# A pinned order for the matmuls of a mixer, weights loaded earlier at the start, and a last norm without GpSimd

## The chip, the core and the metric

The program runs on one core of a Trainium2 chip, as one launch. Its engines are TensorE (PE for the products, PEld for loading their stationary operands), VectorE (DVE), ScalarE (ACT), GpSimd (POOL) and SyncE (SP), which issues most of the DMAs. The metric is the device time of one execution in microseconds (us). The median of three runs of the kernel before is 1447.36 us (1445.93 to 1447.79).

## The reference, cut to what matters

Two layers over 384 tokens (128 of a context group, 256 of a latent group), each layer a half SwiGLU FFN, a token mixer and another half FFN, each with an RMS norm and a shift, scale and gate that come from a condition vector by one matrix per layer. Only the first layer's mixer, the start and the final norm matter here.

```
def _gla_chunked(q, k, v, log_a, s0):            # chunks of 64 tokens, 4 heads, DK 64, DV 128
    b = cumsum(log_a); b_last = b[..., -1:]
    q_dec, k_inv, k_end = q*exp(b), k*exp(-b), k*exp(b_last - b)
    attn    = einsum('thk,shk->hts', q_dec, k_inv) * mask
    o_intra = einsum('hts,shv->thv', attn, v)
    delta   = einsum('shk,shv->hkv', k_end, v)   # the update of one chunk
    S, s_in = scan(S = decay*S + delta)          # the state that each chunk sees, from s0
    o_inter = einsum('thk,hkv->thv', q_dec, s_in)
    return o_intra + o_inter, S

def _gla_fnet_mixer(h, ...):
    q, k, v, og, lf, lb, u = split(h @ w_in)
    o  = rms(gla(forward) + gla(backward), g_head)      # mean over the 128 values of a head
    gla_out = o * silu(og)
    fn_out  = real(fft2(u, axes=(tokens, channels)))    # 4 groups of 128 channels
    return concat([gla_out, fn_out]) @ w_out, s_f, s_b

x = x + 0.5*gate*((silu(h @ w1) * (h @ w3)) @ w2)       # a half FFN, h = rms(x, g)*(1 + scale) + shift
y = rms(x, final_g)
```

## The kernel before, in words

Activations lie transposed, features on the 128 partitions and the 384 tokens along the free axis. A large product is made of three matmuls in a reduced float32 form (fp32r): weight and activation are each split into a high and a low part (`whi`, `wlo`, `hh`, `hl`; ACT makes the high part, DVE the low one), and high by high, high by low and low by high are added up in PSUM (`mm3` and `mm3x`, L345 to L355). Weights come from HBM in units of 1 MB (`raw`), in the order of one list; `load_to` issues the DMAs, `split_to` the split, `take` hands out the next unit. While a half FFN runs, DVE also works out the modulation vectors of later sub-layers by dot products (L151).

The start (L904 to L963) computes the first sub-layer's shift and scale in four quarters q. For each, 32 small matmuls (`mod<-raw_mod`, two tiles of 1 MB) give 512 sums, which are turned (`modt`), added to a bias and used to shift and scale two feature slices of x; those slices are then ready for the first products. Between the quarters stand products of the first two units of `w1` and `w3` (`ffn_p`, 8 slices k of 6 matmuls each), in an order written out in `fill` (L928). The PE order of this part is fixed (`manual_schedule`). x slices, `raw_mod` and the first three weight units share SP's queue.

The first mixer (`mixer_gla_fnet`, from L473) has the projections `in0`, `og`, `v`, `u`, then small matmuls in plain float32: the updates `delta` (L584: 40 of the first kind for ten pairs of chunk and direction, each in fact two passes, 64 rows deep), the scores `at` (L645), the two steps `fa` and `fb` of the Fourier transform (L618, L626), the outputs `o` of a block of 128 tokens (L663 and L669), and the mean of their squares `om` (L673). For each block ACT squares the outputs (`osq`, L671), `rsqrt` (L174 to L186: two ACT, then three DVE instructions on tiles `rs1`, `rs2`, `rs3`, of which `rs1` and `rs3` have one buffer) gives one over the root, and DVE multiplies by it and by the gate (L676, L678) and splits the result for the output projection `out0`. The states go from chunk to chunk by DVE (L597, L599). The order on every engine is set by a scheduler here, which interleaves pieces as it sees them become ready; PSUM has eight banks, from which `one_bank` and `two_banks` take in turn.

The end is `Last` (L239 to L275): the squares of slices 0 to 5 are added up on POOL (`ssq_final`), those of slices 6 and 7 go into the mean's matmuls separately (L267); `put` computes one over the root for the two token groups and multiplies x in pieces, some on DVE and two on POOL (L274), each with a DMA of its own (L275).

Of the kernel before, what the change touches and what calls it, by code (L numbers as in the profile page):

```python
# [9 lines left out]
F32 = mybir.dt.float32  # L10
# [35 lines left out]
def trunk(ctx, tc, a):  # L46
# [192 lines left out]
    class Last(Norm):  # L239
# [22 lines left out]
        def finish(self):  # L262
            terms = [self.ssq] + self.rest
            for c, t0, t1 in GROUPS:
                mean = one_bank(f"mean_final{c}")[:, : t1 - t0]
                for n, t in enumerate(terms):
                    pe.matmul(mean, lhsT=ones, rhs=t[:, t0:t1], start=(n == 0), stop=(n == len(terms) - 1))  # L267
                self.means.append(mean)

        def put(self, c, t0, t1, pieces):  # L270
            r = rsqrt(self.means[c], t1 - t0, f"final{c}")
            for n, (e, d0, d1) in enumerate(pieces):
# [72 lines left out]
    def mm3(out, wh, wl, mh, ml, start, stop):  # L345
        first = pe.matmul(out, lhsT=wh, rhs=mh, start=start, stop=False)  # L346
        pe.matmul(out, lhsT=wh, rhs=ml, start=False, stop=False)  # L347
        pe.matmul(out, lhsT=wl, rhs=mh, start=False, stop=stop)  # L348
        return first
# [8 lines left out]
    def products(pp, u, by_tile=False):  # L358


        for m, k in [(m, k) for k in range(KD) for m in range(2)] if by_tile else [(m, k) for m in range(2) for k in range(KD)]:
            wh, wl = u[m]
            mm3x(pp[:, m], wh[:, k], wl[:, k], k)
# [109 lines left out]
    def mixer_gla_fnet(l, feed, make_next):  # L473
        with tc.tile_pool(name="mix0", bufs=1) as mp, tc.tile_pool(name="mix0w", bufs=2) as mw:
# [32 lines left out]
            for dr in range(2):  # L507
                for pr in range(2):
# [16 lines left out]
                    df = mw.tile([P, T], F32, tag="ke", name=f"df{nm}")  # L525
# [43 lines left out]
            def channels(i):  # L569
                uu.append(tmp.tile([P, 2, T], F32, tag="ev", name=f"u{i}"))  # L570
                project(("u0", i), feed, uu[i], f"u0_{i}")
# [5 lines left out]
            def advance(c, dr, to):  # L577
                t, hf = c // 2, c % 2
                pd = one_bank(f"delta{c}{dr}")
                rows = slice(64 * hf, 64 * hf + 64)  # L580
                for pr in range(2):
                    for par_ in range(2):
                        hd = 2 * pr + par_
                        pe.matmul(  # L584
                            pd[64 * par_ : 64 * par_ + 64, pr * P : pr * P + P],
                            lhsT=kt[rows, t, dr, pr, 64 * par_ : 64 * par_ + 64],
                            rhs=v[rows, t, hd * P : hd * P + P], start=True, stop=True,
                        )
                if to is None or c in (0, 1):
                    s = mp.tile([P, 2, P], F32, name=f"s{c}{dr}")  # L590
                else:
                    s = st[:, 3 * dr + (c - 2) % 3]
                prev = s_in.get((dr, c))
                for pr in range(2):
                    cols = slice(pr * P, pr * P + P)
                    if prev is None:
                        dve.tensor_copy(s[:, pr], pd[:, cols])  # L597
                    else:
                        dve.scalar_tensor_tensor(  # L599
                            s[:, pr], prev[:, pr], dec[dr, pr][:, c : c + 1], pd[:, cols], op0=ALU.mult, op1=ALU.add  # L600
                        )
                if to is not None:
                    s_in[dr, to] = s
                return s
# [10 lines left out]
            def fourier(g):  # L615
# [3 lines left out]
                y = mw.tile([P, 3, 256], F32, tag="fy", name=f"fy{g}", bufs=1)  # L619
                act.copy(y[:, :2].rearrange("p t c -> p (t c)"), pa[:, :512])  # L620
                dve.tensor_tensor(y[:, 2], y[:, 1], pa[:, 512:768], op=ALU.subtract)
                dve.tensor_tensor(y[:, 1], y[:, 1], pa[:, 512:768], op=ALU.add)
                pb = one_bank(f"fb{g}")[:, :T]
# [13 lines left out]
            def scores(t):  # L637
# [12 lines left out]
                w2 = mw.tile([P, 4, P], F32, tag="as", name=f"as{t}")  # L650
# [4 lines left out]
            def attend(t, am):  # L655
                ts = slice(t * P, t * P + P)
                po = two_banks(f"o{t}")
                sq = tmp.tile([P, 2, 256], F32, tag="rs3", name=f"osq{t}", bufs=1)
                todo = [(dr, c) for c in (2 * t, 2 * t + 1) for dr in range(2) if (dr, c) in s_in]
                for pr in range(2):  # L660
                    for par_ in range(2):
                        hd = 2 * pr + par_
                        pe.matmul(po[:, par_, pr * P : pr * P + P], lhsT=v[:, t, hd * P : hd * P + P], rhs=am[:, 2 * par_ + pr],  # L663
                                  start=True, stop=not todo, skip_group_check=True)
                    for n_, (dr, c) in enumerate(todo):
                        o0 = pr * P + (c % 2) * 64
                        for par_ in range(2):
                            rows = slice(64 * par_, 64 * par_ + 64)
                            pe.matmul(po[:, par_, o0 : o0 + 64], lhsT=s_in[dr, c][rows, pr], rhs=qd[dr, pr][rows, c * 64 : c * 64 + 64],  # L669
                                      start=False, stop=(n_ == len(todo) - 1), skip_group_check=True)  # L670
                act.activation(sq, po[:, :, :256], AF.Square)  # L671
                pm = one_bank(f"om{t}")
# [8 lines left out]
            def deltas():  # L681
                for i in range(3):
                    advance(2 + i, 0, 3 + i)
                    advance(5 - i, 1, 4 - i)
                    if i == 0:
                        advance(0, 0, 1)
                        advance(1, 1, 0)
                    if i == 1:
                        nc.sync.dma_start(a["sf"], advance(1, 0, None))
                        nc.sync.dma_start(a["sb"], advance(0, 1, None))  # L690
# [12 lines left out]
            fourier(2)  # L703
            attend(2, am[2])
            fourier(3)
# [200 lines left out]
    with tc.tile_pool(name="boot", bufs=1) as bp, tc.manual_schedule(engines={mybir.EngineType.PE}):  # L906
        raw_mod = {}
        for q in range(4):
# [4 lines left out]
            load_to(min(q + 1, 2))  # L913
# [3 lines left out]
        def begin(ft, ks):  # L917
# [9 lines left out]

        fill = (((), ((0, (0, 1)),)), ((), ((0, (2, 3)), (1, (0, 1)))), (((1, (2,)),), ((1, (3,)), (0, (4, 5)))), (((1, (4,)),), ((1, (5,)), (0, (6, 7)), (1, (6, 7)))))  # L928
        for q in range(4):
# [8 lines left out]
            row = bp.tile([P, P], F32, name=f"modrow0_{q}")  # L938
            dve.tensor_copy(row, acc)
            for args in fill[q][0]:  # L940
                begin(*args)
            pt = one_bank(f"modt0_{q}")
            pe.transpose(pt[:, :P], row, ident)
# [11 lines left out]
            if q < 2:  # L955
                split_to(q + 1)
            for d in (2 * q, 2 * q + 1):
                feed.add(d)
            for args in fill[q][1]:
                begin(*args)  # L960
# [11 lines left out]
    last.put(*GROUPS[0], ((dve, 0, 4), (pool, 4, 8)))  # L972
    last.put(*GROUPS[1], ((dve, 0, 2), (pool, 6, 8), (dve, 2, 4), (dve, 4, 6)))
# [147 lines left out]
```

## Time and profile before

| | us |
|---|---|
| median of three runs | 1447.36 |
| profiled execution | 1448.87 |
| its span | 1446.0 |
| PE busy | 1412.8 (98%) |
| DVE busy | 1086.2 (75%) |
| ACT busy | 599.2 (41%) |
| POOL busy | 125.1 (9%) |

The profiled execution is 2.87 us longer than its span, and 1.51 us longer than the median. PE is busy for almost the whole span, so a stretch of time in which PE waits is what can be seen at once; a wait of another engine matters only where PE waits for that engine in turn. The granted clock is one in most of the span and a half in a few short stretches.

### The profile page before, as it was taken

The numbers are of one execution on the slowest core, as the hardware profiler recorded it, in microseconds if no ns is written. First come the engines' busy times: TensorE is split into PE (matmuls) and PEld (weight loads), VectorE is DVE, ScalarE is ACT, GpSimd is POOL, SyncE is SP. The second block draws the span as 40 slices with busy tenths as digits, with TensorE's granted clock in tenths as the row PEclk, the third lists the DMA queues.
The fourth block names the chain that finished last, engine by engine and source line by source line (L and its number), as shares of the span: only waits on it lengthen the run. The fifth ranks groups of instructions, "written<-read, shape, count | busy, mean of one in ns | idle before, by whom it ended". The sixth has DMA issues, their size and how long they took to land.

```text
span 1446.0 us, 21500 instructions
## 1 busy us (share of the span) xinstructions
PE 1412.8 (98%) x8508; PEld 1371.4 (95%) x8508; DVE 1086.2 (75%) x1815; ACT 599.2 (41%) x976; POOL 125.1 (9%) x98
## 2 busy tenths in 40 slices
PE   6999999999999999999999999999999999999996
PEld 4999999999889999999999999999876999999996
DVE  3799889879876888888879888885667675666433
ACT  4543443335344443433344344333248444344332
POOL 2000000012102000000100000011145200000001
PEclk9999999999999999999999999999989999999998
DMA  9666657563414456556636565664320234433331
GB/s 394 233 212 206 226 185 243 214 218 110 154 47 144 147 198 209 195 188 222 225 132 238 200 204 190 215 219 156 121 85 1 103 132 150 142 131 125 124 103 44
DMA packets 48515, 245.26 MB, mean 170 GB/s; under 512 B 5376, under 2 KB 9856, under 8 KB 29088
## 3 DMA queue, kind: packets, MB, share of 16 engines
q1 hardware_dynamic: 44560, 240.80, 47.6%
q10 hardware_dynamic: 3856, 3.10, 0.7%
q8 instruction: 66, 1.08, 0.3%
q14 instruction: 33, 0.27, 0.1%
HBM read 241.79 MB, written 2.10 MB: 169 GB/s over the span
## 4 chain that ended last, share of the span: by engine, by line
PE 95%; DVE 2%; ACT 1%; DMA 1%; issue 0%; DVEq 0%; SPq 0%; ACTq 0%
PE ffn_p L353 17%; PE ffn_p L355 17%; PE ffn_p L354 17%; PE ffn_acc L346 8%; PE ffn_acc L348 8%; PE ffn_acc L347 8%; PE out_acc L348 2%; PE out_acc L346 2%; PE out_acc L347 2%; PE attn L796 1%; PE av L871 1%; PE attn L851 1%; DMA raw_mod<-in_modw 1%; PE mod L934 1%; PE attn L353 0%; DVE wlo L214 0%
## 5 line engine op out<-in xcount | busy, mean ns | idle before, releaser
L213 ACT CAST whi<-raw 128x1024 fp32r<-128x1024 f32 (+2 forms) x317 | 324.7, 1027 | 609.1 <-PE ffn_p L354 279.9
L214 DVE TENSOR_TENSOR wlo<-raw,whi 128x1024 fp32r<-128x1024 f32 (+2 forms) x317 | 377.8, 1195 | 167.1 <-ACT whi L213 166.3
L353 PE MATMUL ffn_p<-hh,whi 128*128 128x388 f32 x1408 | 478.4, 340 | 4.6 <-ACT whi L213 3.0
L355 PE MATMUL ffn_p<-hh,wlo 128*128 128x386 f32 x1408 | 475.1, 337 | 1.1 <-DVE wlo L214 1.1
L354 PE MATMUL ffn_p<-hl,whi 128*128 128x384 f32 x1408 | 472.7, 336 | 0.2
L151 DVE SCALAR_TENSOR_TENSOR junk<-modw,cb 128x1024 f32<-128x1024 f32 x256 | 314.3, 1228 | 2.1
L353 PEld LDWEIGHTS ffn_p<-hh,whi 128*128 128x128 f32 x1408 | 265.0, 188 | 6.5 <-ACT whi L213 3.2
L355 PEld LDWEIGHTS ffn_p<-hh,wlo 128*128 128x128 f32 x1408 | 265.8, 189 | 2.7 <-DVE wlo L214 2.6
L354 PEld LDWEIGHTS ffn_p<-hl,whi 128*128 128x128 f32 x1408 | 264.6, 188 | 1.4 <-DVE hl L235 1.0
L346 PE MATMUL ffn_acc<-gh_ffn,whi 128*128 128x384 f32 x704 | 236.8, 336 | 0.0
L348 PE MATMUL ffn_acc<-gh_ffn,wlo 128*128 128x384 f32 x704 | 236.7, 336 | 0.0
L347 PE MATMUL ffn_acc<-gl_ffn,whi 128*128 128x384 f32 x704 | 236.7, 336 | 0.0
L203 POOL TENSOR_TENSOR ssq_n<-ssq_n,sq_n 128x384 f32<-128x384 f32 x42 | 59.7, 1423 | 894.0 <-ACT sq_n L202 869.6
L347 PEld LDWEIGHTS ffn_acc<-gl_ffn,whi 128*128 128x128 f32 x704 | 132.4, 188 | 0.0
L346 PEld LDWEIGHTS ffn_acc<-gh_ffn,whi 128*128 128x128 f32 x704 | 132.4, 188 | 0.0
L348 PEld LDWEIGHTS ffn_acc<-gh_ffn,wlo 128*128 128x128 f32 x704 | 132.4, 188 | 0.0
L434 DVE TENSOR_TENSOR ffn_e<-ffn_p,r_n 128x768 f32<-128x768 f32 x88 | 84.0, 955 | 49.1 <-PE ffn_p L355 48.9
L85 ACT ACTIVATE ffn_e<-ffn_e,ffn_wb 128x128 f32<-128x128 f32 (+1 forms) x176 | 70.4, 449 | 51.8 <-DVE ffn_wb L368 51.5
L214 DVE TENSOR_TENSOR gl_ffn<-ffn_e,gh_ffn 128x384 fp32r<-128x384 f32 x88 | 49.0, 557 | 37.6 <-ACT gh_ffn L213 37.4
L213 ACT CAST gh_ffn<-ffn_e 128x384 fp32r<-128x384 f32 x88 | 45.0, 511 | 62.3 <-DVE ffn_e L438 61.8
L438 DVE SCALAR_TENSOR_TENSOR ffn_e<-ffn_e,ffn_wb 128x128 f32<-128x128 f32 (+1 forms) x176 | 65.0, 411 | 0.0
L235 DVE SCALAR_TENSOR_TENSOR hl<-x,mods,hh 128x128 fp32r<-128x128 f32 (+1 forms) x96 | 57.3, 637 | 2.0 <-ACT hh L234 1.2
(261 smaller groups left out, 1256.2 us busy)
## 6 DMA issues: line engine op xcount, KB each, us to landing
raw<-in_w SPq DMA_DIRECT2D x120, 1024.0 KB, 4.8
modw<-in_modw SPq DMA_DIRECT2D x128, 512.0 KB, 3.4
raw<-in_w SPq DMA_DIRECT2D x16, 768.0 KB, 4.9
raw_mod<-in_modw SPq DMA_DIRECT2D x8, 1024.0 KB, 15.3
raw<-in_w_in SPq DMA_DIRECT2D x8, 1024.0 KB, 4.8
raw<-in_w_out SPq DMA_DIRECT2D x8, 1024.0 KB, 4.8
raw<-in_w_og SPq DMA_DIRECT2D x2, 1024.0 KB, 4.7
raw<-in_w_v SPq DMA_DIRECT2D x2, 1024.0 KB, 4.8
```

Source lines behind the costliest of these rows:

```text
L85: i = act.activation(out, in_, func, **kw)
L151: i = dve.scalar_tensor_tensor(junk, raw, 1.0, cb[:, c], op0=ALU.mult, op1=ALU.mult, accum_out=mods[l][v][:, d, c : c + 1])
L213: i = act.copy(hi, src).ins
L214: pace["last"] = dve.tensor_tensor(lo, src, f(hi), op=ALU.subtract).ins
L346: first = pe.matmul(out, lhsT=wh, rhs=mh, start=start, stop=False)
L347: pe.matmul(out, lhsT=wh, rhs=ml, start=False, stop=False)
L348: pe.matmul(out, lhsT=wl, rhs=mh, start=False, stop=stop)
L353: first = pe.matmul(out[:, :TX], lhsT=wh, rhs=hh[:, k, :TX], start=(k == 0), stop=False)
L354: pe.matmul(out[:, :T], lhsT=wh, rhs=hl[:, k], start=False, stop=False)
L355: pe.matmul(out[:, :TM], lhsT=wl, rhs=hh[:, k, :TM], start=False, stop=(k == KD - 1))
L434: dve.tensor_tensor(e, pp[:, :, :T], feed.r.unsqueeze(1).broadcast_to([P, 2, T]), op=ALU.mult)
L438: dve.scalar_tensor_tensor(e[:, 1, t0:t1], e[:, 1, t0:t1], wb[:, 1, c : c + 1], e[:, 0, t0:t1], op0=ALU.add, op1=ALU.mult)
```

## The change

Three places are changed. In the first mixer the PE order is written out and pinned: matmuls of one form stand in runs; all 40 updates stand in one run, between the two halves of the second `u` unit, and take turns between the upper and lower 64 rows; the state chain on DVE follows as one piece; the outputs of blocks 0 and 1 share one pair of PSUM banks (`o01`), and block 2 has another; the Fourier steps are two functions (`by_channel`, `by_token`), and so are the squares and the gate (`squares`, `gated`). The tiles of `df` move to another tag, and the masked scores of the last block take an `rs2` tile. At the start the second unit's weights are loaded right behind the first's, ahead of x's second quarter, and the products are put in another order. At the end slice 6 joins POOL's sum of squares, the means stand behind the last products, and all final multiplications are DVE's.

```
# the end
         def add(self, d):
-            if d < KD - 2:
+            if d < KD - 1:
...
-                    pe.matmul(mean, lhsT=ones, rhs=t[:, t0:t1], start=(n == 0), stop=(n == len(terms) - 1))
+                    i = pe.matmul(mean, lhsT=ones, rhs=t[:, t0:t1], start=(n == 0), stop=(n == len(terms) - 1))
+                    after(i.ins, pace["product"], "the last products before the means")
...
-                e.tensor_tensor(xs, xs, r.unsqueeze(1).broadcast_to([P, d1 - d0, t1 - t0]), op=ALU.mult)
+                dve.tensor_tensor(xs, xs, r.unsqueeze(1).broadcast_to([P, d1 - d0, t1 - t0]), op=ALU.mult)
...
-    last.put(*GROUPS[0], ((dve, 0, 4), (pool, 4, 8)))
-    last.put(*GROUPS[1], ((dve, 0, 2), (pool, 6, 8), (dve, 2, 4), (dve, 4, 6)))
+    last.put(*GROUPS[0], ((0, 4), (4, 8)))
+    last.put(*GROUPS[1], ((0, 2), (2, 4), (4, 6), (6, 8)))
# the mixer
+            def channels(i, between):
                 uu.append(tmp.tile([P, 2, T], F32, tag="ev", name=f"u{i}"))
-                project(("u0", i), feed, uu[i], f"u0_{i}")
+                u = take(("u0", i))
+                pp = two_banks(f"u0_{i}")
+                half(pp, u, 0)
+                between()
+                half(pp, u, 1)
+                spread(uu[i], pp, feed, f"u0_{i}")
+                pump()
...
+                for n in range(0, len(steps), 2):
+                    for pr in range(2):
+                        for par_ in range(2):
+                            for c, dr, to in steps[n : n + 2]:
+                                t, hf = c // 2, c % 2
+                                rows = slice(64 * hf, 64 * hf + 64)
...
-                w2 = mw.tile([P, 4, P], F32, tag="as", name=f"as{t}")
+                if t < 2:
+                    w2 = mw.tile([P, 4, P], F32, tag="as", name=f"as{t}")
+                else:
+                    w2 = tmp.tile([P, 4, P], F32, tag="rs2", name=f"as{t}")
...
-            turn_values(0, vts[0])
-            channels(0)
-            turn_values(1, vts[1])
-            deltas()
-            am = [scores(0), scores(1)]
-            fourier(0)
-            fourier(1)
-            channels(1)
-            attend(0, am[0])
-            am.append(scores(2))
-            attend(1, am[1])
-            fourier(2)
-            attend(2, am[2])
-            fourier(3)
+            with tc.manual_schedule(engines={mybir.EngineType.PE}):
+                turn_values(0, vts[0])
+                channels(0, lambda: turn_values(1, vts[1]))
+                am[0] = scores(0)
+                channels(1, deltas)
+                am[1] = scores(1)
+                am[2] = scores(2)
+                for g in range(2):
+                    y[g] = by_channel(g)
+                pair = two_banks("o01")
+                po[0], po[1] = pair[:, :, :256], pair[:, :, 256:]
+                for t in range(2):
+                    attend(t, am[t], po[t])
+                po[2] = two_banks("o2")[:, :, :256]
+                attend(2, am[2], po[2])
+                for g in range(2):
+                    by_token(g, y[g])
+                gated(0, po[0], squares(0, po[0]))
+                gated(1, po[1], squares(1, po[1]))
+                for g in range(2, 4):
+                    y[g] = by_channel(g)
+                gated(2, po[2], squares(2, po[2]))
+                for g in range(2, 4):
+                    by_token(g, y[g])
# the start
-            load_to(min(q + 1, 2))
+        load(0)
+        load_to(2)
+        for q in range(1, 4):
+            load(q)
         load_to(3)
...
+        sums(0)
+        apply(0)
+        split_to(1)
+        begin(0, 0, 1)
+        split_to(2)
+        begin(1, 0, 1)
+        sums(1)
+        apply(1)
+        sums(2)
+        begin(0, 2)
+        apply(2)
+        begin(0, 3)
+        begin(1, 2, 3)
+        sums(3)
+        begin(0, 4)
+        apply(3)
+        begin(0, 5)
+        begin(1, 4, 5)
+        begin(0, 6, 7)
+        begin(1, 6, 7)
         split_to(3)
```

Below is what the order of instructions says of three places. The first is DVE around the states of the first mixer, before (`at` and `delta` are PSUM tiles of scores and updates, `am` and `as` the masked scores, `states` and `s` the states).

```order
L214 TENSOR_TENSOR wlo_1024_3637<-raw_3331,whi_1024_3636 128x1024
...
L599 SCALAR_TENSOR_TENSOR states<-c_s0f,dec_3029,delta_3489 128x128
...
L649 TENSOR_TENSOR am_3574<-at_3565,c_mask 128x512
L597 COPY s_3508<-delta_3503 128x128 x2
...
L651 TENSOR_TENSOR as_3576<-at_3565,c_mask 128x512
L599 SCALAR_TENSOR_TENSOR states<-states,dec_3029,delta_3519 128x128
...
L649 TENSOR_TENSOR am_3588<-at_3579,c_mask 128x512
...
L651 TENSOR_TENSOR as_3590<-at_3579,c_mask 128x512
```

And the same stretch of DVE now, from the first masked scores to the last.

```order
L680 TENSOR_TENSOR am_3498<-at_3489,c_mask 128x512
L685 TENSOR_TENSOR as_3500<-at_3489,c_mask 128x512
L151 SCALAR_TENSOR_TENSOR junk,mods_7_99<-modw_7_6_3638,cb 128x1024 x2
L214 TENSOR_TENSOR wlo_0_3861<-raw_3421,whi_0_3860 128x1024
L626 SCALAR_TENSOR_TENSOR states<-c_s0f,dec_3029,delta_3539 128x128
...
L380 TENSOR_TENSOR u_3503<-u_1_3514,r_n_2934 128x768
...
L214 TENSOR_TENSOR wlo_1024_3865<-raw_3421,whi_1024_3864 128x1024
...
L680 TENSOR_TENSOR am_3651<-at_3642,c_mask 128x512
L685 TENSOR_TENSOR as_3653<-at_3642,c_mask 128x512
L680 TENSOR_TENSOR am_3665<-at_3656,c_mask 128x512
L685 TENSOR_TENSOR as_3667<-at_3656,c_mask 128x512
```

The scores of blocks 1 and 2 (`at_3642`, `at_3656`) are masked behind the whole state chain, the second `u` unit and the split of two weight tiles; before, blocks 0 and 1 were masked between the steps of the chain.

The second place is PE around the means of squares of the first mixer, before (`osq` are the squared outputs, `fy` the result of the first Fourier step).

```order
L618 MATMUL fa_3781<-c_cc,u_3631 128x256 x3
L673 MATMUL om_3767<-osq_3745,ones_h 128x512
L626 MATMUL fb_3789<-c_cs_p,fy_3785 128x128 x2
L663 MATMUL o_3800<-as_3741,v_3106 128x128 x2
L626 MATMUL fb_3789<-c_cs_s,fy_3785 128x128 x4
...
L618 MATMUL fa_3837<-c_cc,u_3631 128x256 x2
L673 MATMUL om_3823<-osq_3801,ones_h 128x512
L618 MATMUL fa_3837<-c_cc,u_3631 128x256
L346 MATMUL out_acc_3865<-fh,whi_1024_3636 128x384
```

And now.

```order
L657 MATMUL fb_3751<-c_cs_s,fy_3682 128x128 x4
L711 MATMUL om_3764<-osq_3762,ones_h 128x512
L711 MATMUL om_3781<-osq_3779,ones_h 128x512
L646 MATMUL fa_3795<-c_cc,u_3503 128x256 x3
L646 MATMUL fa_3803<-c_cc,u_3503 128x256 x3
L711 MATMUL om_3813<-osq_3811,ones_h 128x512
L657 MATMUL fb_3827<-c_cs_p,fy_3799 128x128 x2
L657 MATMUL fb_3827<-c_cs_s,fy_3799 128x128 x4
L347 MATMUL out_acc_3859<-fh,whi_1024_3508 128x384
```

The three means stand almost together, the first two with nothing between them; before, score, output and Fourier matmuls stood between one mean and the next.

The third place is PE at the end of the program, before.

```order
L348 MATMUL ffn_acc_12491<-gh_ffn_10406,wlo_1024_12553 128x384
L267 MATMUL mean_final_12653<-ssq_final,ones 128x128
L267 MATMUL mean_final_12657<-ssq_final,ones 128x256
L267 MATMUL mean_final_12653<-sq_final_12624,ones 128x128
L346 MATMUL ffn_acc_12491<-gh_ffn_10406,whi_0_12548 128x384
...
L267 MATMUL mean_final_12657<-sq_final_12624,ones 128x256
L267 MATMUL mean_final_12653<-sq_final_12648,ones 128x128
L267 MATMUL mean_final_12657<-sq_final_12648,ones 128x256
```

And now.

```order
L349 MATMUL ffn_acc_12485<-gh_ffn_10400,wlo_1024_12547 128x384
L267 MATMUL mean_final_12647<-ssq_final,ones 128x128
L267 MATMUL mean_final_12650<-ssq_final,ones 128x256
L267 MATMUL mean_final_12647<-sq_final_12642,ones 128x128
L267 MATMUL mean_final_12650<-sq_final_12642,ones 128x256
```

All matmuls of the mean stand behind the last product, and there are four of them in place of six.

## Rows read from the trace of the kernel before

**Rows 1.** The page: shares of the span of the chain that ended last, by engine.

```profile
PE 95%; DVE 2%; ACT 1%; DMA 1%; issue 0%; DVEq 0%; SPq 0%; ACTq 0%
```

**Rows 2.** PE in order of time, the mixer: start, length, instruction, idle time before it.

```profile
376.46 0.82 PE L554 MATMUL vt<-ident,vT 128*128 128x128 f32 x6
...
400.42 0.61 PE L663 MATMUL o<-as,v 128*128 128x128 f32 x4
...
403.55 1.13 PE L673 MATMUL om<-osq,ones_h 128*128 128x512 f32 x2 [0.20 <-ACT osq L671]
...
408.79 1.53 PE L618 MATMUL fa<-c_cc,u 128*128 128x256 f32 x6
410.16 1.02 PE L673 MATMUL om<-osq,ones_h 128*128 128x512 f32 x2
...
452.88 0.34 PE L353 MATMUL ffn_p<-hh,whi 128*128 128x388 f32 x1
```

**Rows 3.** DVE in order of time, the same stretch.

```profile
377.61 1.22 DVE L214 TENSOR_TENSOR wlo<-raw,whi 128x1024 fp32r<-128x1024 f32 x1
378.74 1.02 DVE L376 TENSOR_TENSOR u<-u,u_wb 128x256 f32<-128x256 f32 x2
379.68 0.60 DVE L599 SCALAR_TENSOR_TENSOR states<-c_s0f,dec,delta 128x128 f32<-128x128 f32 x2
...
389.16 1.22 DVE L151 SCALAR_TENSOR_TENSOR junk<-modw,cb 128x1024 f32<-128x1024 f32 x1
...
406.76 0.68 DVE L649 TENSOR_TENSOR am<-at,c_mask 128x512 f32<-128x512 f32 x1
```

**Rows 4.** ACT in order of time, the first block's squares and root.

```profile
404.77 0.69 ACT L85 ACTIVATE lnv_o<-om,eps 128x512 f32<-128x512 f32 x1 [1.28 <-PE om L673]
...
409.34 0.60 ACT L671 ACTIVATE osq<-o 128x512 f32<-128x512 f32 x1 [3.21 <-DVE r_o L186]
```

**Rows 5.** POOL in order of time, the masked scores' sums.

```profile
387.17 1.27 POOL L652 TENSOR_TENSOR as<-as,am 128x512 f32<-128x512 f32 x1 [3.03 <-DVE as L651]
```

**Rows 6.** Stretches: length; PE, PEld, DVE, ACT, POOL busy; clock; DMA share, GB/s.

```profile
1043.00:1045.70 2.70, 0.95 (x12) 0.57 (x8) 2.70 (x3) 0.00 (x0) 2.27 (x2) 0.99 0.00 0
1045.70:1052.50 6.80, 6.45 (x18) 5.43 (x19) 4.09 (x6) 1.58 (x9) 2.54 (x2) 0.50 0.46 157
...
1072.80:1076.40 3.60, 0.26 (x2) 0.26 (x4) 3.60 (x10) 2.44 (x7) 1.26 (x1) 1.00 0.63 264
1076.40:1079.80 3.40, 3.40 (x14) 1.62 (x14) 2.87 (x12) 1.84 (x7) 2.67 (x3) 0.50 0.00 0
```

**Rows 7.** PE in order of time, the start.

```profile
30.55 1.95 PE L934 MATMUL mod<-raw_mod,cs 128*32 128x128 f32 x64
...
46.69 0.34 PE L353 MATMUL ffn_p<-hh,whi 128*128 128x388 f32 x1
46.87 0.34 PE L354 MATMUL ffn_p<-hl,whi 128*128 128x384 f32 x1
...
48.23 0.45 PE L355 MATMUL ffn_p<-hh,wlo 128*128 128x386 f32 x1 [0.50 <-DVE wlo L214]
```

**Rows 8.** SP's DMA issues in order of time, the start.

```profile
8.14 2.26 SPq L912 DMA_DIRECT2D raw_mod<-in_modw  x2
```

**Rows 9.** The tile raw_mod, its DMAs' times from issue to landing.

```profile
DMA to landing us min/median/max: 6.4/15.3/18.0
```

**Rows 10.** All engines in order of time, the end.

```profile
1429.05 0.82 PE L267 MATMUL mean_final<-ssq_final,ones 128*128 128x128 f32 x4
...
1430.30 0.42 PE L346 MATMUL ffn_acc<-gh_ffn,whi 128*128 128x384 f32 x1
...
1436.86 1.71 POOL L274 TENSOR_TENSOR x<-x,r_final 128x512 f32<-128x512 f32 x1 [22.88 <-ACT r_final L85]
...
1437.82 1.04 DVE L185 SCALAR_TENSOR_TENSOR u_final<-u_final,r_final 128x256 f32<-128x256 f32 x1
...
1439.35 2.96 DVE L274 TENSOR_TENSOR x<-x,r_final 128x512 f32<-128x512 f32 x3
```

More of the change, by code (lines that the diff above doesn't have):

```diff
@@ L347, in mm3 @@
         pe.matmul(out, lhsT=wh, rhs=ml, start=False, stop=False)
-        pe.matmul(out, lhsT=wl, rhs=mh, start=False, stop=stop)
+        pace["product"] = pe.matmul(out, lhsT=wl, rhs=mh, start=False, stop=stop).ins
         return first
@@ L362, in products, with half @@
             wh, wl = u[m]
+            mm3x(pp[:, m], wh[:, k], wl[:, k], k)
+    def half(pp, u, m):
+        wh, wl = u[m]
+        for k in range(KD):
             mm3x(pp[:, m], wh[:, k], wl[:, k], k)
@@ L507, in mixer_gla_fnet @@
             for dr in range(2):
+                kes = mw.tile([P, 2, T], F32, tag="fy", name=f"df{dr}")
                 for pr in range(2):
@@ L524, in mixer_gla_fnet @@
                     bl = b6[:, :, 0:1] if dr else b6[:, :, 63:64]
-                    df = mw.tile([P, T], F32, tag="ke", name=f"df{nm}")
+                    df = kes[:, pr]
                     pool.tensor_tensor(df.rearrange("p (c t) -> p c t", c=6), bl.broadcast_to([P, 6, 64]), b6, op=ALU.subtract)
@@ L575, in mixer_gla_fnet @@
             s_in = {(0, 2): cst["s0f"], (1, 5): cst["s0b"]}
[L577 to L597, printed above, removed]
-                    else:
[L599 to L604, printed above, removed]
@@ L622, in fourier, with by_token @@
                 dve.tensor_tensor(y[:, 1], y[:, 1], pa[:, 512:768], op=ALU.add)
+                return y
+            def by_token(g, y):
                 pb = one_bank(f"fb{g}")[:, :T]
@@ L653, in scores, with attend @@
                 return w2
[L655 to L658, printed above, removed]
+            def attend(t, am, po):
                 todo = [(dr, c) for c in (2 * t, 2 * t + 1) for dr in range(2) if (dr, c) in s_in]
@@ L663, in attend @@
                         pe.matmul(po[:, par_, pr * P : pr * P + P], lhsT=v[:, t, hd * P : hd * P + P], rhs=am[:, 2 * par_ + pr],
-                                  start=True, stop=not todo, skip_group_check=True)
+                                  start=True, stop=False, skip_group_check=True)
                     for n_, (dr, c) in enumerate(todo):
@@ L670, in attend, with squares, gated @@
                                       start=False, stop=(n_ == len(todo) - 1), skip_group_check=True)
+            def squares(t, po):
+                sq = tmp.tile([P, 2, 256], F32, tag="rs3", name=f"osq{t}", bufs=1)
                 act.activation(sq, po[:, :, :256], AF.Square)
+                return sq
+            def gated(t, po, sq):
+                ts = slice(t * P, t * P + P)
                 pm = one_bank(f"om{t}")
@@ L906, in trunk, with load @@
     with tc.tile_pool(name="boot", bufs=1) as bp, tc.manual_schedule(engines={mybir.EngineType.PE}):
-        raw_mod = {}
-        for q in range(4):
+        raw_mod, rows = {}, {}
+        def load(q):
             nc.sync.dma_start(x[:, 2 * q : 2 * q + 2], a["xT"][:, 2 * q : 2 * q + 2])
@@ L925, in begin, with sums @@
                     mm3x(begun[ft][:, i], wh[:, k], wl[:, k], k)
-        fill = (((), ((0, (0, 1)),)), ((), ((0, (2, 3)), (1, (0, 1)))), (((1, (2,)),), ((1, (3,)), (0, (4, 5)))), (((1, (4,)),), ((1, (5,)), (0, (6, 7)), (1, (6, 7)))))
-        for q in range(4):
+        def sums(q):
             acc = one_bank(f"mod0_{q}")[:, :P]
@@ L937, in trunk, with apply @@
                         )
[L938 to L941, printed above, removed]
+            rows[q] = bp.tile([P, P], F32, name=f"modrow0_{q}")
+            dve.tensor_copy(rows[q], acc)
+        def apply(q):
             pt = one_bank(f"modt0_{q}")
-            pe.transpose(pt[:, :P], row, ident)
+            pe.transpose(pt[:, :P], rows[q], ident)
             for v in range(2):
```

56 lines of the change are left out of this document (37 added, 19 removed).

## The prediction

> **What bounds the kernel now.** I read the chain that ended last first: 95% of it is PE's [rows 1], so the end moves by what PE's stream gains or loses, and by the short stretches at the two ends where PE has nothing to do. The second view is PE in order of time through the first mixer. It shows hardly a gap: 0.20 us before the first mean of squares is the kind of wait to be found there, though the chain from one mean to the next is long. From the first `om` to the second are 410.16 - 403.55 = 6.6 us [rows 2], in which PE does scores, outputs and a Fourier step. The scheduler had put work there. Third, DVE in the same stretch, since the new order makes PE wait for it [rows 3], and ACT's part of the root [rows 4]. Fourth, the stretches with the granted clock, for what happens after PE has been idle. Last, the start and the end, where the page's share of PE says nothing.
>
> **The mixer up to the outputs.** PE does the same until the first `vt`. Its second one (0.82 us long, of which 0.75 hold up what follows, [rows 2]) now stands inside the first `u` unit, so DVE has that unit 0.75 us later: its last additions, 378.74 to 379.68 before [rows 3], end at 380.4. What DVE then does is fixed by its order. Two masks of the first scores at 0.60 (a 512-wide one is 0.68 long and overlaps the next by some 0.08) bring it to 381.6; two dots and one weight split, each 1.13 to 1.15 from start to start (377.61 to 378.74), to 385.05. Then the chain: 16 multiply-adds at 0.26 (two in 0.52, 0.60 long) and four copies, which I take at 0.2, end at 390.0. The second `u` unit's scaling with the weight split and the additions behind it takes what the first's took, 3.1 us from the product's end (376.46, by the `vt` behind it) to 379.68 less the latency: 393.1. Masks of block 1: 394.3. The masked part of block 2 needs the single `rs1` tile, which POOL reads for 1.27 us [rows 5]: 395.6, and two masks more: 396.8.
>
> PE is ahead of that. By the runs' own durations it has done the scores of block 2 and the first `fa` by 392.5. The second `fa` takes over the PSUM bank of block 1's scores and waits for 394.3: 1.9 us idle. The outputs' bank pair takes over that of block 2's scores: PE is free at 395.7 and waits until 397.0 with the semaphore: 1.3 us. So whatever PE saves by runs of one form before 397.0, it waits away; the shorter updates gain nothing. Outputs began at 400.42 before and at 397.0 now.
>
> **The mixer from there.** Before, 452.88 - 400.42 = 52.5 us led to the next FFN [rows 2]. Of these 0.5 us were waits and 1.3 us the scores of block 2, which now lie earlier; 2.4 us of `fb` for two groups, which stood among the products of `u`, come in. So 53.1 us of work, and I take 0.3 us off for fewer changes of form (0 to 1.5: the outputs keep their alternation of forms, so little is left to save).
>
> The Trainium skill, "TensorEngine Tiling (Array Packing)", section Key Properties, says that a change of the tiling mode drains TensorE, by which each change taken out should pay. It does here too, but those taken out lie mostly ahead of the wait that ends at 397.0.
>
> Now the waits. The first `om` waits 0.15 us for a PSUM bank. The second stands directly behind it, and its squares on ACT wait for DVE's last reading of block 0's output: `rs3` has one buffer. Before, that chain took 6.6 us with two masks of 0.60 inside, so 5.4; the squares waited for the third instruction of the root (409.34, [rows 4]) and now for the product behind it, 0.7 us more: 6.1 us from `om` to `om`. The mean itself is 0.9 of that: PE idles 5.2 us. Behind it come `om` and one `fa` (1.4 us for six, [rows 2]); the next `fa` has the same PSUM bank and waits until DVE has made `fy` from the one before, which in DVE's order stands behind block 1's root: 1.3 us until the logarithm, 0.7 and 0.6 on ACT, five DVE instructions of 0.7 (three of 512 columns) or 0.45 (my estimate for the two of 256), in all 5.7 us from the second `om`, of which 2.3 are work: 3.4 us idle. The last `fb` waits 0.2 us. Products of `out0` behind that have only six matmuls of cover in front of `fb`, yet what they read is ready about in time. Waits: 0.15 + 5.2 + 3.4 + 0.2 = 9.0. The FFN starts at 397.0 + 53.1 - 0.3 + 9.0 = 458.8, against 452.88: **+5.9 us** (+2 to +8).
>
> **The clock.** After PE had been idle for 3.34 of 3.60 us the granted clock was 0.50 for the next 3.4 us; after 1.75 of 2.70 us it was 0.50 for 6.8 us [rows 6], that is 1.2 GHz. At the half clock the work of such a stretch costs its half: 1.7 to 3.4 us. The 5.2 us wait makes the second `om` 0.9 us longer, which the chain behind hands on; the `fa` is hidden in the next wait. After the 3.4 us wait I take 2.6, the middle. **+3.5 us** (0 to +7; the upper end if the two waits before 397.0 also count).
>
> The Trainium skill, "TensorE: Matmul & The Clock Gate", section What's actually happening, has a monitor that halves the clock after idleness and restores it after activity; the two pairs of stretches agree. By the page alone the sum stays as it is.
>
> **The start.** Loads from x's third quarter on keep their place. The tile for the third quarter's sums, issued between 8.14 and 10.40 [rows 8], lands at most 18.0 us later [rows 9]: I take 28.0. Before, the sums began at 30.55 and the two units were through at 46.87, 16.3 us later [rows 7]. Now 12 matmuls more stand behind, 2.1 us at 0.18 from start to start, so they are through at 46.4; the wait of 0.50 at 48.23 goes, since its split starts earlier, and some 0.3 of idle time between quarters. **-1.3 us** (-3.5 to +1: the mean is now last, and its root on ACT and DVE has the third unit's products as cover; without that cover some 2 us).
>
> **The end.** The six matmuls of the mean held up the products from 1429.05 to 1430.30, 1.25 us [rows 10]. Behind that, DVE's 1.04 us instruction lies beside POOL's 1.71 us one; alone I take 0.4 as for the others, -0.65. DVE gets one multiplication more for the first group, +0.6, and four at 0.6 for the second, 2.4 against 2.96. The last one ends 1.25 + 0.65 - 0.6 + 0.55 = 1.85 earlier: **-1.8 us** (-0.8 to -2.2).
>
> **Sum.** 5.9 + 3.5 - 1.3 - 1.8 = +6.3 us on the profiled execution's 1448.87: 1455.2. That execution was 1.51 above the median, so I predict 1453.7.
>
> **Rivals.**
> 1. The clock does not fall, or falls where a wait follows: +2.8, 1450.2, at the very bound of what can be told from no change (0.2%, 2.9 us). For it: dense work stands on both sides of each wait, and part of the half-clocked work lies in the next wait. Against: 5.2 us is longer than the idle time of either stretch above.
> 2. The clock falls at every wait, those before 397.0 too, and DVE is later by a POOL addition: +6.3 + 2.5 + 0.8, 1457. The pair of 1.9 and 1.3 us in 4.5 us lies near the 1.75 in 2.70 that did it.
> 3. Not slower: DVE reaches the masks of blocks 1 and 2 in time. The place is the two waits before 397.0. If dots and splits lie outside the way of the chain, PE runs through to the outputs at 393.8, 3.2 us earlier, and its run stays dense, so that only the 5.2 us wait touches the clock (+0.9): 5.9 - 3.2 + 0.9 - 3.1 = +0.5, 1447.9. With the start and the saved changes of form at their good ends it is 1444. It decides from 3.4 us of gain against my sum (1453.7 - 1450.3). Against it: DVE's order puts three 1.15 us instructions ahead of the chain.
> 4. The order does less than written, as the waits come from banks other than I take them: no place for it in the order of PE and ACT.
>
> **How the numbers follow.** The forecast 0.47, own range 1450.5 to 1457; rival 1 0.19, its lower half within 0.2%; rival 2 0.13; rival 3 0.15, a third of it faster; unforeseen 0.06, evenly. Faster by over 0.2% (below 1444.5): 0.09. Within: 0.27. Slower (above 1450.3): 0.64. The range leaves out a tenth at either end: 1445 to 1459.
>
> **What would show it.** In the profile after: a PE idle of about 5 us before the second `om` named to ACT's `osq`, one of about 3 us before an `fa` named to DVE's `fy`, and 1 to 2 us each before an `fa` and the first `o`; the clock at a half behind them; `ffn_p` after the mixer about 6 to 9 us later by the distance from the first `vt`; no `mean_final` among the last products and no POOL product behind them. If the two long waits are missing, the forecast is wrong by their size; if they are there and the time is not longer, the savings in the runs were worth more than I gave them.

## The result, and the profile after

The changed kernel takes 1453.39 us (median of 7 runs, 1450.12 to 1459.28) against 1447.36 (7 runs, 1445.43 to 1447.79). The ratio over all runs is 1.0055, with a 95% interval of 1.0033 to 1.0077. The two medians alone give 1.0042, since three of the seven runs are long ones, of 1457.8 to 1459.3 us with a mean granted clock of 0.985 to 0.986, against 0.991 to 0.993 in the other four. It is slower, by 6.0 us by the medians and by 4.8 to 11.1 by the interval. The forecast was 1453.7. The profiled execution took 1453.39 itself, with a span of 1451.3 us.

First, PE in order of time through the first mixer of the changed kernel (start, length, instruction, idle time before it), beside [rows 2].

```profile
364.21 0.42 PE L354 MATMUL u<-hh,whi 128*128 128x388 f32 x1
...
379.01 2.42 PE L609 MATMUL delta<-v,kt 64*64 64x128 f32 x80
...
387.48 1.16 PE L676 MATMUL at<-qd,ki 64*128 64x128 f32 x16 [0.56 <-DVE states L626]
388.57 1.56 PE L646 MATMUL fa<-c_cc,u 128*128 128x256 f32 x6
391.77 1.53 PE L646 MATMUL fa<-c_cc,u 128*128 128x256 f32 x6 [1.64 <-DVE as L685]
394.44 0.68 PE L694 MATMUL o<-as,v 128*128 128x128 f32 x4 [1.14 <-DVE as L685]
...
406.61 1.10 PE L711 MATMUL om<-osq,ones_h 128*128 128x512 f32 x2
412.73 2.08 PE L711 MATMUL om<-osq,ones_h 128*128 128x512 f32 x2 [5.03 <-ACT osq L705]
414.60 2.77 PE L646 MATMUL fa<-c_cc,u 128*128 128x256 f32 x6
419.52 2.90 PE L646 MATMUL fa<-c_cc,u 128*128 128x256 f32 x6 [2.15 <-DVE fy L650]
...
460.81 0.34 PE L354 MATMUL ffn_p<-hh,whi 128*128 128x388 f32 x1
```

The five waits of 0.56, 1.64, 1.14, 5.03 and 2.15 us are the new ones, 10.5 us in all, and each names the engine that ends it. Behind the 5.03 us wait the same instructions take about twice as long: `om` 2.08 us in place of 1.10 before it, `fa` 2.77 in place of 1.56. The stretches show the clock (length; PE, PEld, DVE, ACT, POOL busy; clock; DMA).

```profile
407.00:412.70 5.70, 0.70 (x2) 0.00 (x0) 4.01 (x7) 2.05 (x4) 0.00 (x0) 0.90 0.00 0
412.70:419.50 6.80, 4.63 (x8) 2.53 (x9) 3.69 (x8) 2.94 (x5) 0.00 (x0) 0.50 0.00 0
419.50:426.00 6.50, 6.48 (x21) 4.93 (x22) 3.22 (x6) 2.70 (x5) 0.00 (x0) 0.56 0.00 0
```

From 412.7 to about 425 the clock is at a half. The chain behind the 5 us wait stands on ACT and, for the instruction that releases the squares, on DVE (the two views, in that order):

```profile
407.80 0.69 ACT L85 ACTIVATE lnv_o<-om,eps 128x512 f32<-128x512 f32 x1 [0.66 <-PE om L711]
...
412.08 0.60 ACT L705 ACTIVATE osq<-o 128x512 f32<-128x512 f32 x1 [2.93 <-DVE r_o L714]
```

```profile
410.63 0.69 DVE L186 SCALAR_TENSOR_TENSOR r_o<-u_o,r_o 128x512 f32<-128x512 f32 x1
411.36 0.69 DVE L714 TENSOR_TENSOR r_o<-o,r_o 128x512 f32<-128x512 f32 x1
```

In [rows 4] the squares of the second block were released by L186; now it is the product behind it. Block 2, which has a bank pair of its own, is still released by L186 in the same trace:

```profile
419.08 0.60 ACT L705 ACTIVATE osq<-o 128x512 f32<-128x512 f32 x1 [1.09 <-DVE r_o L186]
```

Ahead of the outputs one instruction of DVE takes 0.96 us longer than the dot in front of it (1.22 us), while POOL's addition beside it takes 0.92 more than in [rows 5]:

```profile
379.08 2.18 DVE L151 SCALAR_TENSOR_TENSOR junk<-modw,cb 128x1024 f32<-128x1024 f32 x1
377.98 2.19 POOL L686 TENSOR_TENSOR as<-as,am 128x512 f32<-128x512 f32 x1 [25.65 <-DVE as L685]
```

The start and the end gained, as these rows show (PE at the start, then PE and DVE at the end, beside [rows 7, 10]).

```profile
26.29 1.08 PE L975 MATMUL mod<-raw_mod,cs 128*32 128x128 f32 x32
27.54 1.08 PE L975 MATMUL mod<-raw_mod,cs 128*32 128x128 f32 x32 [0.17 <-DMA raw_mod<-in_modw]
```

```profile
1435.19 0.34 PE L349 MATMUL ffn_acc<-gh_ffn,wlo 128*128 128x384 f32 x1
1435.56 0.74 DVE L402 SCALAR_TENSOR_TENSOR x<-ffn_acc,mods,x 128x128 f32<-128x128 f32 x2 [10.27 <-PE ffn_acc L349]
1436.36 0.45 PE L347 MATMUL ffn_acc<-gh_ffn,whi 128*128 128x384 f32 x1 [0.83 <-DVE x L402]
...
1444.51 0.42 DVE L185 SCALAR_TENSOR_TENSOR u_final<-u_final,r_final 128x256 f32<-128x256 f32 x1
...
1445.42 2.50 DVE L275 TENSOR_TENSOR x<-x,r_final 128x512 f32<-128x512 f32 x4
```

Where the time went, by the start of the same instruction in both traces:

| stretch | before | after | difference |
|---|---|---|---|
| start to the first `u` product | 367.92 | 364.21 | -3.7 |
| first `u` product to the next FFN | 84.96 | 96.60 | +11.6 |
| that FFN to the last product | 980.45 | 978.61 | -1.8 |
| last product to the end of the last multiplication | 8.98 | 8.50 | -0.5 |

The sum is +5.6; the spans differ by 5.3. Of the -1.8 in the third line only 0.2 lie at the means of the end; 1.6 lie in the second mixer, which was not changed (from its `in_q` products behind `v1t` to the mean of the next norm it takes 139.41 us before and 137.80 after).

### The profile page after: what moved, and what is told of

Its sections match the earlier page's. It is cut to its first block, busy times and chain, and to the rows that moved or that the text cites. A ratio compares the mean times of both kernels' runs of the same rounds, so it can differ in the third digit from the quotient of the medians.

```text
span 1451.3 us, 21480 instructions
## 1 busy us (share of the span) xinstructions
PE 1411.3 (97%) x8504; PEld 1371.4 (94%) x8504; DVE 1085.6 (75%) x1817; ACT 599.4 (41%) x975; POOL 122.2 (8%) x97
## 4 chain that ended last, share of the span: by engine, by line
PE 94%; DVE 2%; DMA 2%; ACT 1%; issue 0%; POOL 0%; SPq 0%; DVEq 0%; ACTq 0%
PE ffn_p L354 17%; PE ffn_p L356 17%; PE ffn_p L355 17%; PE ffn_acc L347 8%; PE ffn_acc L348 8%; PE ffn_acc L349 8%; DMA raw_mod<-in_modw 2%; PE out_acc L349 2%; PE out_acc L347 2%; PE out_acc L348 2%; PE attn L834 1%; PE av L909 1%; PE attn L889 1%; PE fb L657 0%; PE attn L354 0%; PE og L354 0%
```

## The experiments

**The mixer alone.** The mixer as changed, with the start and the end of the kernel before.

```
-            if d < KD - 1:
+            if d < KD - 2:
...
-        load(0)
-        load_to(2)
...
+            load_to(min(q + 1, 2))
...
-    last.put(*GROUPS[0], ((0, 4), (4, 8)))
+    last.put(*GROUPS[0], ((dve, 0, 4), (pool, 4, 8)))
```

> The mixer's new order alone, with the start and the end of the kernel before. Theory (the mixer's waits and the clock behind them cost what the trace of after shows, 11.7 us from the first product of u to the next FFN, and the start and end give 5.5 back): 1447.4 + 11, between 1455 and 1462. Rival (part of the loss comes from the earlier arrival at the mixer or lies elsewhere): 1450 to 1454.

1457.66 us against 1447.33 (ratio 1.0071, 1.0057 to 1.0086). The rows of PE at the mixer's two ends:

```profile
369.17 0.42 PE L353 MATMUL u<-hh,whi 128*128 128x388 f32 x1
...
465.71 0.34 PE L353 MATMUL ffn_p<-hh,whi 128*128 128x388 f32 x1
```

96.54 us between them, as in the changed kernel: the whole loss is in the mixer, and it is the same when the mixer is reached 5 us later.

**The start and the end alone.** The reverse: the mixer of before, the rest as changed.

```
-            with tc.manual_schedule(engines={mybir.EngineType.PE}):
-                turn_values(0, vts[0])
-                channels(0, lambda: turn_values(1, vts[1]))
...
+            turn_values(0, vts[0])
+            channels(0)
+            turn_values(1, vts[1])
+            deltas()
...
```

> The new start and the new end alone, with the mixer of before. Theory (3.7 us at the start by the distance to later products, 1.7 at the end): 1442, between 1440.5 and 1444; the products of the first mixer start about 3.7 us earlier than in before. Rival (the gain at the start was this one execution's clock, or is lost again where later loads are waited for): 1445 to 1447.

1443.53 us (ratio 0.9977, 0.9967 to 0.9987): these two parts are a gain of about 3.8 us, near the 4.4 of the trace (3.7 at the start, 0.7 at the end). The mixer takes 84.97 us there (364.35 to 449.32), as in before.

**Filling the waits.** Matmuls of no use, on constant operands, in front of the second and the third mean.

```
+                for _ in range(n):       # n = 5 ahead of the second mean, 2 of the third
+                    pe.matmul(pm, lhsT=ones_h, rhs=cb[:, 0, :512], start=True, stop=True)
```

> The changed kernel with matmuls of no use (constant operands, a result that is overwritten) in front of the second and the third mean of squares: five where PE idled 5.0 us and two where it idled 2.2 us. Everything else waits as before. Theory (part of the loss is the half clock behind the waits): the granted clock stays at 1.0 from 407 to 430 and the time falls by 2.5 to 4.5 us, to about 1450. Rival (the chain on ACT and DVE alone sets the time there): unchanged within 1 us, or later by the filling.

1449.39 us (ratio 1.0021, 1.0010 to 1.0031), 4.0 less than the changed kernel, for seven matmuls more. PE, and below it the stretches:

```profile
406.81 1.10 PE L718 MATMUL om<-osq,ones_h 128*128 128x512 f32 x2
408.15 4.53 PE L711 MATMUL om<-cb,ones_h 128*128 128x512 f32 x10 [0.24 <-DVE fl L662]
412.94 1.12 PE L718 MATMUL om<-osq,ones_h 128*128 128x512 f32 x2 [0.26 <-ACT osq L705]
413.90 1.46 PE L646 MATMUL fa<-c_cc,u 128*128 128x256 f32 x6
415.20 1.88 PE L711 MATMUL om<-cb,ones_h 128*128 128x512 f32 x4
417.58 1.53 PE L646 MATMUL fa<-c_cc,u 128*128 128x256 f32 x6 [0.50 <-DVE fy L650]
```

```profile
407.00:413.00 6.00, 5.50 (x13) 1.96 (x12) 4.09 (x7) 2.26 (x5) 0.00 (x0) 1.00 0.00 0
413.00:419.80 6.80, 6.30 (x20) 3.76 (x21) 4.76 (x10) 3.71 (x7) 0.00 (x0) 1.00 0.00 0
```

From mean to mean it is 6.13 us, as it was 6.12: the chain is the same, so the filling hid nothing and cost nothing. But the clock stays at one, and the mixer takes 91.69 us (364.42 to 456.11) in place of 96.60. Of the 11.6 us lost in the profiled execution, 6.7 are the waits against what the order saves, and 4.9 the half clock.

**Another buffer for the squares.** They take the masked scores' two buffers, free by then, in place of `rs3`.

```
-                sq = tmp.tile([P, 2, 256], F32, tag="rs3", name=f"osq{t}", bufs=1)
+                sq = mw.tile([P, 4, P], F32, tag="as", name=f"osq{t}") ...
```

> The changed kernel with the squares of a block in the buffers of the masked scores (two, free by then) in place of the single buffer that the root shares. Theory (the 5.0 us wait is the single buffer; behind it stands the chain of roots on DVE, which the next Fourier step waits for): the second mean follows the first at once, but the wait before the second Fourier step of the second unit grows from 2.2 us to 5 to 7, the clock still falls once, and 1 to 3.5 us are won: about 1451. Rival (buffer alone was the bound): all 5 us and the clock come back, 1445 to 1447.

Neither came: 1454.22 us (1.0053, 1.0039 to 1.0067), and the same wait, to the hundredth (PE, then ACT).

```profile
412.79 2.07 PE L711 MATMUL om<-osq,ones_h 128*128 128x512 f32 x2 [5.03 <-ACT osq L705]
```

```profile
412.14 1.09 ACT L705 ACTIVATE osq<-o 128x512 f32<-128x512 f32 x2 [2.94 <-DVE r_o L714]
```

The single buffer alone is not what holds the second block's squares. They wait for L714, the product that reads block 0's outputs, though it touches neither the new buffer nor block 1's values. What the two share is the PSUM tile `o01`. That this is the cause is a conclusion from what is left; block 2 speaks for it: its squares, on a pair of their own, waited for L186 alone while they had the old buffer, and here they follow block 1's at once (the second of the two in the row).

**The squares written down first.** With that buffer, the squares of both blocks are issued ahead of DVE's product.

```
+                sq = [squares(t, po[t]) for t in range(2)]
                 for g in range(2):
                     by_token(g, y[g])
-                gated(0, po[0], squares(0, po[0]))
-                gated(1, po[1], squares(1, po[1]))
+                gated(0, po[0], sq[0])
+                gated(1, po[1], sq[1])
```

> The run with own buffers for the squares showed the same 5.03 us wait, released by DVE's product that reads block 0's output. Here the squares of blocks 0 and 1 are also issued ahead of that product, right behind the outputs. Theory (two things hold the second block's squares: the buffer, and the bank pair that both blocks share, whose readers go in the order in which they are written down): the second mean follows the first without a wait; the next Fourier step then waits some 5 us in place of 2.2, behind both roots on DVE; one fall of the clock in place of two; the mixer from the first product of u to the next FFN gets 4 to 7 us shorter than 96.6, the time about 1447 to 1450. Rival (the bank pair is not what holds it): the 5.0 us wait stays and so does the time.

1448.45 us (1.0013, 1.0004 to 1.0022), 5 us less.

```profile
408.11 1.10 PE L711 MATMUL om<-osq,ones_h 128*128 128x512 f32 x2 [0.23 <-DVE fl L662]
...
415.11 2.35 PE L646 MATMUL fa<-c_cc,u 128*128 128x256 f32 x6 [4.61 <-DVE fy L650]
```

The 5.03 us wait is gone, and the one behind it has grown from 2.15 to 4.61, as block 0's root and gate and the first two instructions of block 1's root now stand ahead of `fy` on DVE. One half-clocked stretch is left, and the mixer takes 91.14 us. So half of what the first wait gave back is waited for at the second. The new order of writing was not run with the old buffer, so that the share of each is not separated.

**Scores earlier, dots later.** Block 1's scores ahead of the second `u` unit, and the two modulation dots not in front of the state chain.

```
                 am[0] = scores(0)
+                am[1] = scores(1)
                 channels(1, deltas)
-                am[1] = scores(1)
...
-                pump()
+                if i == 0:
+                    pump()
```

> The changed kernel with the scores of block 1 ahead of the second u unit and the two modulation dots behind the outputs, so that DVE masks block 1 ahead of the state chain; the rest of the order as it is. Theory (the 0.56, 1.64 and 1.14 us waits before the outputs are DVE's order): they shrink to about 1.2 in all, the outputs start 2 to 3 us earlier by the distance from the first product of u, and the time falls by as much, to about 1450.5; the 5 and 2 us waits and the half clock stay. Rival (what is won there is waited away behind): outputs earlier, next FFN at the same distance.

The waits before the outputs shrink from 3.34 to 1.74 us, where 1.2 were expected:

```profile
388.15 2.83 PE L647 MATMUL fa<-c_cc,u 128*128 128x256 f32 x12 [0.23 <-PE at L677]
392.49 0.68 PE L695 MATMUL o<-as,v 128*128 128x128 f32 x4 [1.51 <-DVE as L686]
```

The outputs start 28.17 us behind the first `u` product (364.32), in place of 30.23, and the mixer takes 94.60, 2.0 less. The time, 1451.78 us (1.0043, 1.0026 to 1.0060), is 1.6 less; its runs spread from 1449.05 to 1461.21, so that the time alone would not show it.

**Both, and the chain hidden.** Outputs and Fourier steps stand between the means again, in a pinned order. The earlier scores, the later dots and the squares' other buffer are in it too.

```
+                attend(0, am[0], po[0])
+                sq = [squares(0, po[0])]
+                y[2] = by_channel(2)
+                attend(1, am[1], po[1])
+                sq.append(squares(1, po[1]))
+                gated(0, po[0], sq[0])
+                by_token(0, y[0])
                 po[2] = two_banks("o2")[:, :, :256]
                 attend(2, am[2], po[2])
...
+                gated(1, po[1], sq[1])
+                by_token(1, y[1])
+                y[3] = by_channel(3)
                 gated(2, po[2], squares(2, po[2]))
```

> Both, and a pinned order in which outputs and Fourier steps stand between the means of squares again: outputs 0, Fourier step, outputs 1, mean 0, Fourier step, outputs 2, mean 1, two Fourier steps, mean 2. Theory (runs of one form are worth 3 to 5 us of PE time once no wait eats them): the mixer takes 81 to 83 us from the first product of u to the next FFN, against 85.0 in before and 96.6 in the changed kernel, no wait over 1.5 us, full clock, and the time is 1439 to 1442. Rival (runs of one form are worth nothing, the waits were all there was): 84 to 86 us and 1443 to 1445, as with the start and end alone.

1442.10 us (0.9964, 0.9952 to 0.9976): faster than the kernel before and than the changed one, and by its median than the start and end alone, though those two intervals overlap. It is a tenth of a us above the range expected.

```profile
401.18 1.12 PE L712 MATMUL om<-osq,ones_h 128*128 128x512 f32 x2
...
406.74 1.13 PE L712 MATMUL om<-osq,ones_h 128*128 128x512 f32 x2
...
412.51 0.68 PE L658 MATMUL fb<-c_cs_p,fy 128*128 128x128 f32 x4 [1.16 <-DVE fl L663]
```

The mixer takes 82.95 us (365.92 to 448.87) with 2.9 us of waits (0.23, 1.51 and 1.16), against 84.96 in before with about 1. Without waits that is 80.05 against some 84: the order is worth 4 us of PE time, of which the changed order's waits and half clock leave nothing. By distances from start to start, 2.6 of the 4 us are the 80 passes of the updates (2.3 us in one run, 5.0 scattered before) and 1.05 the scores (3.2 and 4.2). The updates were changed in two ways, one run and row halves in turn, and no run separates the two.

**Three more looks at the changed kernel**, for its spread.

> The changed kernel once more, one execution, for its spread of 1450 to 1459. Theory: in the long executions the clock falls once more in the mixer, at the two waits before the outputs (394 us in the trace), which a short execution passes at full clock: 3 to 6 us more between the first product of u and the next FFN than 96.6. Rival: the spread lies at the start or in the second mixer, and the first mixer takes 96.6 in all of them.

> The changed kernel, a second look at the same question: theory, the mixer takes 96.6 us in a short execution and 100 to 103 in a long one; rival, 96.6 in all.

> The changed kernel, a third look at the same question: theory, the mixer takes 96.6 us in a short execution and 100 to 103 in a long one; rival, 96.6 in all.

1450.79, 1450.18 and 1451.73 us, all near the short end. The first mixer takes 93.85, 93.85 and 95.08 us, in place of 96.60. Both the theory and the rival are wrong for these executions. The waits are the same 5.03 and 2.15 us in the first of them, and only the length of the half-clocked stretch differs:

```profile
413.54 2.08 PE L711 MATMUL om<-osq,ones_h 128*128 128x512 f32 x2 [5.03 <-ACT osq L705]
415.41 2.77 PE L646 MATMUL fa<-c_cc,u 128*128 128x256 f32 x6
420.33 1.53 PE L646 MATMUL fa<-c_cc,u 128*128 128x256 f32 x6 [2.16 <-DVE fy L650]
```

Here the clock is back for the second `fa` (1.53 us, 2.90 in the first trace). No look fell on an execution of 1457 us or more; by the granted clock of those three in the result they spent more time at the half clock, and where they did stays open.

## Why the prediction was right, step by step

*The chain from mean to mean*: right. A PE idle of 5.2 us was forecast, named to the squares, and 5.03 was measured. The price was right and its cause half right: the step named the one buffer `rs3`. With another buffer the wait did not move; it went when the squares were also written down ahead of the other reader of the shared PSUM tile.

*The wait for `fy`*: mis-sized, 2.15 us against 3.4, and not by the clock: at full clock the same place is 2.38 us (1.88 of filling and 0.50 of wait). The sum had 5.7 us from the second `om` to this `fa`, with both instructions for `fy` behind block 1's root on DVE. With the waits filled it is 4.64 (417.58 - 412.94), and DVE does them among the three of the root (at 416.09 and 417.02, the root's last at 417.35). In the trace of after the half-clocked `om` and `fa` take 1.0 and 1.3 us longer, and nearly all of that delays `fy` too, which is made from that `fa`.

*The waits before the outputs*: 1.64 and 1.14 us against 1.9 and 1.3, and one more of 0.56 before block 2's scores, which wait for the end of the state chain. The outputs start 30.2 us behind the first `u` product; the sum had 29.1 (397.0 - 367.92). That they are DVE's order was shown: with scores and dots moved they shrink. Of the 1.1 us that were missed, 0.96 are the dot of 2.18 us beside POOL's addition, in every trace with this order; the sum took 1.15 for it, and only rival 2 had DVE later by an addition of POOL's (0.8).

*The work behind*: right. From the outputs to the FFN the sum had 61.8 us at full clock; with the waits filled it is 456.11 - 394.65 = 61.5.

*The clock*: the mechanism right, the size low in this execution. 3.5 us were forecast (0 to 7); the four traces of the changed kernel have 93.85 to 96.60 us in the mixer against 91.69 at full clock, so 2.2 to 4.9. The forecast took 0.9 us behind the first long wait and 2.6 behind the second; in the first trace the half-clocked stretch runs through both, from 412.7 to about 425. The rule that the forecast took from [rows 6], that such a wait is followed by the half clock, did not hold for the first pair of those rows in the trace of after, as the last section shows.

*The start*: mis-sized, -3.7 us against -1.3 with a range to -3.5. The term counted all of the third quarter's sums from the landing of its second tile, 28.0. That tile was waited for at 27.54, but the first half of the sums (0.9 us) ran ahead of it from 26.29, and the 16.3 us taken over from before held more lost time between its quarters than the 0.3 allowed: three groups of three products, from 34.23, 35.21 and 42.54, took 0.98 to 0.99 us each in place of 0.53. By executions the gain varies: the first `u` product of the changed start is at 364.2 to 365.9 in the traces, that of before at 367.9 and 369.2.

*The end*: wrong in its larger term. 1.25 us were forecast for the six matmuls of the mean among the products, and 0.6 behind them. The second is right (0.5). But the matmuls had stood in a wait: the products behind them take over PSUM from slice 6's, which DVE still reads. Before, this DVE instruction was:

```profile
1429.25 0.74 DVE L396 SCALAR_TENSOR_TENSOR x<-ffn_acc,mods,x 128x128 f32<-128x128 f32 x2 [10.27 <-PE ffn_acc L348]
```

It ended at 1429.99, and the products went on at 1430.30 [rows 10]. With the matmuls gone, PE waits 0.83 us for the same instruction and goes on 0.06 behind its end. From the last product of slice 6 to the next it is 1.17 us in place of 1.43: 0.26 are won, and the end is worth 0.7 us in all, under the -0.8 of the range.

*What the sum did not have*: -1.6 us in the second mixer, which is not touched. It has a half-clocked stretch in the trace of before, behind two waits of DVE's `qs` [rows 6]; in that of after the same waits are there and the matmuls behind them run at full pace, while the half clock behind the later wait of 3.35 us lasts longer. So I put the difference down to the clock, as an argument and not as shown.

In the sum the terms that were off cancel: the start (-2.4), the second mixer (-1.6), the first mixer with its clock (+2.2) and the end (+1.1). The slowdown in the first mixer was forecast by its mechanism, and that the median met the forecast to 0.3 us is luck.

## What to carry to other kernels

A pinned order takes from the scheduler the one thing that hid a long chain: other work between two links. Before matmuls are sorted by form, write down the chain that each of them feeds on the other engines, and keep at least its length of work in between; here 6 us of chain stood behind each mean, and the sorted order left 0.9. A wait of PE can cost more than its length, where the clock falls behind it, so that useless matmuls can make a kernel faster (here by 4.0 us). Work that stands where its engine would wait anyway is worth little to take out: six matmuls that held PE for 1.25 us gave back 0.26. And blocks that share a PSUM tile may have their readers wait for one another, even where no value is shared.

## What the runs showed of the hardware

The granted clock's row seems to miss a fall at times. At the start of the changed kernel it is 1.00 while the products stand 0.32 us apart. In the trace of before they stand at the same distance where the row says 0.51, and 0.18 is the full pace (the stretch of before, then that of after with two of its products):

```profile
14.80:21.70 6.90, 5.92 (x36) 4.58 (x40) 2.63 (x3) 2.47 (x4) 2.73 (x2) 0.51 1.03 429
```

```profile
15.85:23.66 7.81, 7.56 (x24) 6.49 (x24) 4.62 (x4) 4.68 (x7) 4.21 (x4) 1.00 1.01 423
```

```profile
20.67 0.53 PE L354 MATMUL ffn_p<-hh,whi 128*128 128x388 f32 x1
20.99 0.52 PE L355 MATMUL ffn_p<-hl,whi 128*128 128x384 f32 x1
```

So the distance between starts is worth reading beside the row. The same waits can also go either way. In the second mixer, which is the same in both kernels, they are 1.04 and 1.06 us before, and 1.04 and 1.05 after:

```profile
1044.29 0.71 PE L792 MATMUL attn<-kr,qs 64*128 64x128 f32 x6 [1.04 <-DVE qs L376]
1046.05 2.05 PE L729 MATMUL rotq<-qs,c_rot 128*128 128x256 f32 x4 [1.06 <-DVE qs L376]
```

```profile
1052.20 0.71 PE L830 MATMUL attn<-kr,qs 64*128 64x128 f32 x6 [1.04 <-DVE qs L382]
1053.97 1.10 PE L767 MATMUL rotq<-qs,c_rot 128*128 128x256 f32 x4 [1.05 <-DVE qs L382]
```

Before, the four matmuls behind the second wait took 2.05 us, at a granted clock of 0.50 [rows 6]; after, they took 1.10.

Last, DVE and POOL can hold one another up. In the changed kernel an addition on POOL (1.27 us in [rows 5]) and a dot on DVE (1.22 us for the one before it) stand beside each other and take 2.19 and 2.18 us. With the dots moved, a weight split on DVE takes 2.10 us beside such an addition, in place of 1.22.
